# Decoder trunk on one core: means of squares as two products of a rounded part and the rest

## The chip, the cores and the metric

The kernel runs on one core of a Trainium2 chip. The metric is the device time of one execution in microseconds (us); lower is better. The names of the engines are those of the profile: PE (TensorE products), PEld (its weight loads), DVE (VectorE), ACT (ScalarE), POOL (GpSimd) and SP (the queue that issues most transfers).

## What is computed

One inference step of a one-layer decoder trunk, for a prompt of 256 tokens and eight samples of eight tokens each (320 columns in all). Everything is single precision at its borders:

```
h = RMSNorm(x); u = h @ w_in
y = x + (sigmoid(m_A) * (GDN(u) @ w_branch_a) + sigmoid(m_B) * (NSA(u) @ w_branch_b)) @ w_out
```

Mixer A (GDN) is a gated delta rule with 32 value heads. Mixer B (NSA) is sparse attention with 16 query heads and 4 key heads of 128: compressed blocks of keys, 16 selected blocks, and a window of 512. Two norms of mixer B matter here:

```
q  = rmsnorm(q_raw, q_norm_g)                               # 16 heads
kc = rmsnorm(compress(kc_full, pe_k, w_k, proj_k), k_gain)  # compressed keys
rmsnorm(x, g) = x * rsqrt(mean(x * x) + 1e-6) * g
```

## The kernel before

The 128 features of a head lie in the partitions, so a mean over features is a product with a 128x128 matrix of 1/128 on PE. A product can take plain single precision (F32) operands or F32R ones, rounded by ACT as they are written. The large projections take three F32R products a tile: weights rounded (`whi`) by the input rounded (`hhi`), `whi` by the input's rest (`hlo`), and the weights' rest (`wlo`) by `hhi`. They write `acc`. There are 11952 of them, and they are called the **fillers** below, since the order puts them wherever PE would wait.

The work comes in stages: (1) the norm of x and tables; (2) `prepare` (queries and keys of prompt and samples), `compressed` (the compressed keys of the eight samples, one after the other), `prompt` and `window`; (3) the selected blocks of the samples, in two streams (`sample`, called here the sample stage), which reads 256 pages of 256 KB as `spg`; (4) the delta rule, begun by `g_init`, which loads `c_gdn`, `c_gini` and others; (5) the last projections. The streams are generators. `Run` picks at each step the stream that a clock of estimated costs (`Clock`, `Timed`) lets start first, and so fixes, while the program is built, one order of instructions for each engine. The engines then run their own lists in that order, held by semaphores.

Projections wait in a list `Q`. `p_load` brings weights (`wraw`, three buffers) by SP, `p_hi` rounds them on ACT (`whi`), `p_lo` takes the rest on DVE (`wlo`), and `p_mm` makes the products. Until stage 3 is over, `Q` holds 99 column tiles of 48 products, 4752 fillers. The projections of the delta rule are put on the list only when the last sample is done, and after them, in the program's order, `g_init` starts.

`rstd` is the generator that both norms call. With `exact` set (16 query heads of 320 columns in `prepare`; eight samples of 512 columns in `compressed`) it multiplies the F32 `mean` by the F32 squares, in one product, and puts one Newton step behind. Without it (eight heads of other keys, one product of the prompt's compressed keys) it rounds the squares on ACT (`sqh`), takes the rest on DVE (`sql`), and makes two F32R products with `meanr`.

Of the kernel before, what the change touches and what calls it, by code (L numbers as in the profile page):

```python
# [10 lines left out]
F32 = mybir.dt.float32  # L11
F32R = mybir.dt.float32r
I32 = mybir.dt.int32
AF = mybir.ActivationFunctionType
OP = mybir.AluOpType
# [6 lines left out]
P = 128  # L22
# [424 lines left out]
def step(ctx: ExitStack, tc: tile.TileContext, I, O):  # L447
# [3 lines left out]
    V, S, G_, T, SY = (Timed(e, n, clock) for e, n in ((nc.vector, "dve"), (nc.scalar, "act"), (nc.gpsimd, "pool"), (nc.tensor, "pe"), (nc.sync, "sp")))  # L451
# [4 lines left out]
    def pool(cx, name, bufs=1, space=None, **kw):  # L456
        if space is not None:
            kw["space"] = space
        return Pool(cx.enter_context(tc.tile_pool(name=name, bufs=bufs, **kw)), name, bufs, clock, space is PSUM)
# [162 lines left out]
    for ti, (t0, n) in enumerate(TT):  # L622
# [3 lines left out]
        if ti == 0:  # L626
            K = load_pack(const, "const")
            ident, mean, one = K["ident"], K["mean"], K["one"]
    meanr = const.tile([P, P], F32R, name="meanr")
# [235 lines left out]
    for nm in ("k_win", "v_win"):  # L865
        G_.dma_start(O["p_" + nm][0, :256].rearrange("(a t) g d -> t a (g d)", a=2), zero)

    def rstd(pl, pp, tag, src, n, exact, tags=("sq", "rs", "nt")):

        sq = pl.tile([P, n], F32, tag=tags[0], name="sq", bufs=1)  # L870
        yield ("act", src)
        S.activation(sq, src, AF.Square)
        if exact:
            yield "pe"
            ms = pp.tile([P, 512], F32, tag=tag, name="ms")
            T.matmul(ms[:, :n], mean, sq, start=True, stop=True)
        else:
            hi, lo = (pl.tile([P, n], F32R, tag=t, name=t, bufs=1) for t in ("sqh", "sql"))
            yield "act"
            S.activation(hi, sq, AF.Copy)  # L880
            yield "dve"
            V.tensor_tensor(lo, sq, hi.bitcast(F32), op=OP.subtract)
            yield ("pe", lo, Next(pp, tag))
            ms = pp.tile([P, 512], F32, tag=tag, name="ms")
            T.matmul(ms[:, :n], meanr, hi, start=True, stop=False)
            T.matmul(ms[:, :n], meanr, lo, start=False, stop=True)
        yield "act"
        r = pl.tile([P, n], F32, tag=tags[1], name="rs", bufs=1)
        S.activation(r, ms[:, :n], AF.Ln, bias=eps)
        yield "act"  # L890
        S.activation(r, r, AF.Exp, scale=-0.5)
        yield "dve"
        if exact:
            a, b = exact
            t = pl.tile([P, b - a], F32, tag=tags[2], name="nt", bufs=1)
            V.tensor_tensor(t, r[:, a:b], r[:, a:b], op=OP.mult)
            V.scalar_tensor_tensor(t, ms[:, a:b], EPS, t, op0=OP.add, op1=OP.mult)
            yield "dve"
            V.tensor_scalar(t, t, -0.5, 1.5, op0=OP.mult, op1=OP.add)
            V.tensor_tensor(r[:, a:b], r[:, a:b], t, op=OP.mult)  # L900
            yield "dve"
        return r
# [219 lines left out]
    cp = pool(c_ctx, "cp", side="right")  # L1122
    cps = pool(c_ctx, "cps", 2, PSUM, side="right")
# [62 lines left out]
    def qT(b, g):  # L1186
        return qs[:, b, 4 * g:4 * g + 4, :].rearrange("p h t -> p (h t)")

    def pooled(b, kv):
        pp = cps.tile([P, 512], F32, tag="a", name="pp")  # L1190
        for i in range(0, 4, 2):
            pg = []
            for _ in range(8):
                pg.append((yield from cfeed.get()))
            yield ("tiles", *pg)
            for k in range(8):
                j = k % 4
                T.matmul(pp[32 * j:32 * j + 32], Pk[:, kv, i + k // 4], pg[k], start=i + k // 4 == 0, stop=i + k // 4 == 3)
            if i == 0:
                for j in range(3):  # L1200
                    T.matmul(pp[32 * j:32 * j + 32], Pk[:, kv, 4], pg[j + 1], start=False, stop=False)
            cfeed.release(8)
        yield "dve"
        pl = cp.tile([P, 512], F32, tag="c0", name="pl", bufs=1)
        V.tensor_tensor(pl.rearrange("p (g d) -> p g d", g=4), pp.rearrange("p (g d) -> p g d", g=4),
                        bc(cb[:, kv], [[0, 4], [1, P]]), op=OP.add)
        yield ("pe", clock.last, Next(cps, "a"))
        tp = cps.tile([P, 512], F32, tag="a", name="tp")
        for g in range(4):
            T.transpose(tp[:, g * P:g * P + P], pl[:, g * P:g * P + P], ident)  # L1210
        yield "act"
        pt = cp.tile([P, 512], F32, tag="c1", name="pt", bufs=1)
        S.activation(pt, tp, AF.Copy)
        yield "pe"
        return pt

    def compressed():
        for b in range(B):
            pt = yield from pooled(b, 0)
            yield lambda: done["q"] == 16  # L1220
            yield ("pe", clock.last, Next(cps, "a"))
            kp = cps.tile([P, 512], F32, tag="a", name="kp")
            T.matmul(kp, proj[:, 0], pt, start=True, stop=True)
            rs = yield from rstd(cp, cps, "a", kp, 512, (0, 512), ("c0", "c2", "c3"))
            kc = cp.tile([P, 512], F32, tag="c0", name="kc", bufs=1)
            V.scalar_tensor_tensor(kc, kp, gains[:, 1:2], rs, op0=OP.mult, op1=OP.mult)
            yield ("tiles", clock.last, Next(cps, "a"))
            sc = cps.tile([P, 512], F32, tag="a", name="sc")
            for g in range(4):
                T.matmul(sc[32 * g:32 * g + 32, :127], qT(b, g), kc[:, g * P:g * P + 127], start=True, stop=True)  # L1230
            yield "dve"
            s1 = cp.tile([P, 127], F32, tag="s1", name="s1")
            V.scalar_tensor_tensor(s1, sc[:, :127], SCALE, cmpB[:, :127], op0=OP.mult, op1=OP.add)
            mx = cp.tile([P, 3], F32, tag="mxc", name="mxc")
            V.tensor_reduce(mx[:, 0:1], s1, axis=AX.X, op=OP.max)
            V.tensor_scalar(mx[:, 0:1], mx[:, 0:1], -1.0, None, op0=OP.mult)
            yield "act"
            S.activation(s1, s1, AF.Exp, bias=mx[:, 0:1], accum_out=mx[:, 1:2])
            yield "dve"
            V.reciprocal(mx[:, 2:3], mx[:, 1:2])  # L1240
            V.tensor_scalar(s1, s1, mx[:, 2:3], None, op0=OP.mult)
            yield ("pe", clock.last, Next(cps, "a"))
            ip = cps.tile([P, 512], F32, tag="a", name="ip")
            q = 32 * (b % 4)
            T.matmul(ip[q:q + 32, :127], N["G"], s1, start=True, stop=True)
            T.transpose(ip[:127, P:2 * P], s1, ident)
            yield "dve"
            V.tensor_copy(imp[q:q + 32, b // 4, :127], ip[q:q + 32, :127])
            sT = cp.tile([P, P], F32, tag="sT", name="sT")
            V.tensor_copy(sT[:127], ip[:127, P:2 * P])  # L1250
            if b % 4 == 3:
                yield from select(b // 4)
                done["sel"] = b // 4 + 1
            pt = yield from pooled(b, 1)
            vp = cps.tile([P, 512], F32, tag="a", name="vp")
            for g in range(4):
                T.matmul(vp[:, g * P:g * P + P], pt[:, g * P:g * P + P], proj[:, 1], start=True, stop=True)
            yield "dve"
            vc = cp.tile([P, 512], F32, tag="c0", name="vc", bufs=1)
            V.tensor_copy(vc, vp)  # L1260
            yield ("tiles", clock.last, Next(cps, "a"))
            oc = cps.tile([P, 512], F32, tag="a", name="oc")
            for g in range(4):
                T.matmul(oc[32 * g:32 * g + 32, :P], sT[:127, 32 * g:32 * g + 32], vc[:127, g * P:g * P + P], start=True, stop=True)
            yield "dve"
            add_o(oc, gS[:, 0, b:b + 1], b)
            done["cmp"] = b + 1
# [152 lines left out]
    def add_o(x, g, b):  # L1420

        if b in seen:
            V.scalar_tensor_tensor(osum[:, b], x[:, :P], g, osum[:, b], op0=OP.mult, op1=OP.add)
        else:
            V.tensor_scalar(osum[:, b], x[:, :P], g, None, op0=OP.mult)
        seen.add(b)

    run.add(prompt())
    run.add(compressed(), CR)
    run.go(lambda: done["names"])  # L1430
    p_ctx.close()
# [948 lines left out]
```

## Time and profile before

| | us |
|---|---|
| median of 3 runs | 2538.18 |
| lowest, highest | 2533.05, 2538.55 |
| profiled execution: its time | 2536.51 |
| profiled execution: its span, first to last instruction | 2534.7 |
| busy in that span: PE / PEld / DVE / ACT / POOL | 2504.5 / 2337.8 / 1636.3 / 1398.0 / 414.1 |

The profile gives the busy time of each engine. The start of one product is also the moment at which PE took it up, so what a product costs PE is read from start to start; its own duration overlaps with the next. Time that PE stands idle is 30.2 us of the span.

### The profile page before, as it was taken

How to read it: one execution, taken by the hardware profiler on the slowest of the kernel's cores; microseconds unless marked ns; L12 is line 12 of the kernel's file. 1: busy time of each engine (PE TensorE's matmuls, PEld its weight loads, DVE VectorE, ACT ScalarE, POOL GpSimd, SP SyncE). 2: the span in 40 equal slices, each digit the busy share in tenths (PEclk: the TensorE clock that was granted, in tenths of full speed). 3: DMA queues.
4: the chain of work that ended last, by engine and by line, in shares of the span. 5: the costliest groups of instructions: out<-in, count | busy, mean ns of one | idle time of the engine just before them, and what ended most of it. 6: DMA issues, size and time to landing. Idle time of an engine off the chain costs nothing.

```text
span 2534.7 us, 59791 instructions
## 1 busy us (share of the span) xinstructions
PE 2504.5 (99%) x22405; PEld 2337.8 (92%) x22405; DVE 1636.3 (65%) x4075; ACT 1398.0 (55%) x3268; POOL 414.1 (16%) x992
## 2 busy tenths in 40 slices
PE   9999999999999999999999998999999999999999
PEld 8898789888888999999999998999999989999999
DVE  5554446655665555545888878889787876555543
ACT  4553444443444444435778776877877765544443
POOL 2000001000000000001223233433323432000000
PEclk9999999999999999999999999999999999999999
DMA  7657776888886999967455554554665556666564
GB/s 217 236 160 247 243 253 218 291 304 287 308 267 221 328 316 324 314 213 227 140 166 176 184 172 133 181 181 155 185 185 165 168 187 220 217 182 188 182 197 128
DMA packets 553827, 549.15 MB, mean 217 GB/s; under 512 B 33009, under 2 KB 457138, under 8 KB 553154
## 3 DMA queue, kind: packets, MB, share of 16 engines
q1 hardware_dynamic: 538690, 496.30, 61.4%
q0 software_dynamic: 14848, 49.04, 5.4%
q8 instruction: 177, 2.90, 0.5%
q14 instruction: 112, 0.92, 0.1%
HBM read 472.93 MB, written 72.29 MB: 215 GB/s over the span
## 4 chain that ended last, share of the span: by engine, by line
PE 89%; DVE 4%; issue 3%; DMA 2%; ACT 1%; POOL 1%; SPq 0%; DVEq 0%; ACTq 0%; POOLq 0%
PE acc L331 64%; PE ps L331 6%; PE nt L331 4%; PE op L331 3%; PE pp L331 3%; PE ns L331 2%; PE tp L331 2%; PE sp L331 1%; PE bank L331 1%; PE p L331 1%; PE pu L331 1%; PE ms L331 1%; POOL vx L331 1%; DVE wlo L331 1%; PE nought L331 0%
## 5 line engine op out<-in xcount | busy, mean ns | idle before, releaser
L331 PE MATMUL acc<-hhi,whi 128*128 128x320 f32 (+1 forms) x3472 | 1141.3, 329 | 0.6 <-ACT hhi L331 0.6
L331 PE MATMUL acc<-hlo,whi 128*128 128x320 f32 (+1 forms) x3472 | 1073.0, 309 | 1.2 <-DVE hlo L331 1.0
L331 PE MATMUL acc<-hhi,wlo 128*128 128x320 f32 (+1 forms) x3472 | 1073.8, 309 | 0.1
L331 ACT ACTIVATE whi<-wraw 128x512 fp32r<-128x512 f32 (+1 forms) x996 | 625.6, 629 | 812.7 <-PE acc L331 760.1
L331 DVE TENSOR_TENSOR wlo<-wraw,whi 128x512 fp32r<-128x512 f32 x992 | 682.1, 691 | 515.1 <-ACT whi L331 494.6
L331 PEld LDWEIGHTS acc<-hhi,whi 128*128 128x128 f32 (+1 forms) x3472 | 654.4, 188 | 25.1 <-issue 17.0
L331 PEld LDWEIGHTS acc<-hlo,whi 128*128 128x128 f32 (+1 forms) x3472 | 654.7, 189 | 8.7 <-issue 2.4
L331 PEld LDWEIGHTS acc<-hhi,wlo 128*128 128x128 f32 (+1 forms) x3472 | 652.2, 188 | 0.0
L331 PE MATMUL acc<-oah,whi 128*128 128x320 f32 x512 | 158.2, 309 | 0.0
L331 PE MATMUL acc<-oal,whi 128*128 128x320 f32 x512 | 158.2, 309 | 0.0
L331 PE MATMUL acc<-oah,wlo 128*128 128x320 f32 x512 | 158.2, 309 | 0.0
L331 POOL CAST vx<-v 32x128 fp32r<-32x128 f32 x256 | 94.9, 371 | 125.7 <-DVE v L331 88.5
L331 DVE SCALAR_TENSOR_TENSOR cv<-xp,cw,cv 128x344 f32<-128x344 f32 x192 | 110.0, 574 | 8.2 <-ACT cv L331 5.9
L299 POOL DMA_DIRECT2D d_mz<-raw x48 | 26.4, 550 | 493.7 <-ACT raw L331 411.6
L331 PEld LDWEIGHTS acc<-oah,whi 128*128 128x128 f32 x512 | 96.1, 188 | 0.0
L331 PEld LDWEIGHTS acc<-oal,whi 128*128 128x128 f32 x512 | 96.1, 188 | 0.0
L331 PEld LDWEIGHTS acc<-oah,wlo 128*128 128x128 f32 x512 | 96.1, 188 | 0.0
L331 ACT ACTIVATE kT<-nt 128x512 f32<-128x512 f32 x80 | 46.8, 594 | 82.1 <-PE nt L331 81.6
L331 DVE SCALAR_TENSOR_TENSOR sS<-sS,ends,pu 128x128 f32<-128x128 f32 x256 | 84.2, 338 | 11.3 <-PE pu L331 10.4
L331 DVE COPY kT<-nt 128x512 f32<-128x512 f32 x80 | 54.4, 689 | 51.1 <-PE nt L331 50.1
L331 PE MATMUL pp<-cpg,Pk 128*32 128x512 f32 x608 | 76.6, 597 | 0.0
L331 PE MATMUL nt<-pk_const,spg 128*128 128x128 f32 x512 | 73.3, 275 | 2.7 <-DMA spg<-cache_k_sel 2.7
(428 smaller groups left out, 3428.4 us busy)
## 6 DMA issues: line engine op xcount, KB each, us to landing
wraw<-w_in SPq DMA_DIRECT2D x120, 1024.0 KB
wraw<-w_in SPq DMA_DIRECT2D x129, 512.0 KB
cpg<-cache_k_cmp SPq DMA_DIRECT2D x128, 256.0 KB
cpg<-cache_v_cmp SPq DMA_DIRECT2D x128, 256.0 KB
spg<-cache_k_sel SPq DMA_DIRECT2D x128, 256.0 KB
spg<-cache_v_sel SPq DMA_DIRECT2D x128, 256.0 KB
wraw<-w_branch_a SPq DMA_DIRECT2D x32, 1024.0 KB
sS<-state_gdn SPq DMA_DIRECT2D x32, 512.0 KB
```

The lines of the kernel that those rows point to most:

```text
L299: return f(*a, **k)
L331: return f(*a, **k)
```

## The change

`rstd` always takes the way with two F32R products; `exact` now only says which columns get the Newton step. The compressed keys hand in names of buffers that are already there (`c2`, `c3`) for the rounded squares and the rest.

```diff
-    def rstd(pl, pp, tag, src, n, exact, tags=("sq", "rs", "nt")):
+    def rstd(pl, pp, tag, src, n, exact, tags=("sq", "rs", "nt", "sqh", "sql")):
...
-        if exact:
-            yield "pe"
-            ms = pp.tile([P, 512], F32, tag=tag, name="ms")
-            T.matmul(ms[:, :n], mean, sq, start=True, stop=True)
-        else:
-            hi, lo = (pl.tile([P, n], F32R, tag=t, name=t, bufs=1) for t in ("sqh", "sql"))
...
+        hi, lo = (pl.tile([P, n], F32R, tag=t, name=t, bufs=1) for t in tags[3:])
+        yield "act"
+        S.activation(hi, sq, AF.Copy)
+        yield "dve"
+        V.tensor_tensor(lo, sq, hi.bitcast(F32), op=OP.subtract)
+        yield ("pe", lo, Next(pp, tag))
+        ms = pp.tile([P, 512], F32, tag=tag, name="ms")
+        T.matmul(ms[:, :n], meanr, hi, start=True, stop=False)
+        T.matmul(ms[:, :n], meanr, lo, start=False, stop=True)
...
-            rs = yield from rstd(cp, cps, "a", kp, 512, (0, 512), ("c0", "c2", "c3"))
+            rs = yield from rstd(cp, cps, "a", kp, 512, (0, 512), ("c0", "c2", "c3", "c2", "c3"))
```

Since the order follows from estimated costs, the change moves instructions on every engine up to the start of the delta rule; from the product with `gg` on (the second that reads the table `pk_gini`) the order on PE is the same in both. Counted in the two orders, the fillers that stand ahead of four places on PE are:

| place on PE | fillers ahead, before | fillers ahead, now |
|---|---|---|
| first `mp` (start of the sample stage) | 3516 | 3744 |
| last `tp` of `o` (end of the sample stage) | 4659 | 4752 |
| `bank` of `bag` (first use of `pk_gini`) | 4782 | 4788 |
| `bank` of `gg` | 4818 | 4818 |

PE at the end of the sample stage, before. `ns` are scores, `nt` transposes of the softmax `xs`, `op` products with pages `spg`, `tp` the last transpose, `c4` a constant of the delta rule.

```order
L331 MATMUL op_15794<-spg_15944,pT_15994 32x128 x4
L331 MATMUL op_15794<-spg_15946,pT_15994 32x128 x4
L331 MATMUL acc_15851<-hhi_84,whi_15852 128x320
...
L331 MATMUL acc_16017<-hhi_84,wlo_15914 128x320
L331 MATMUL tp_16023<-pk_const_108,o_16012 128x128
L331 MATMUL acc_16017<-hhi_84,whi_15906 128x320
...
L331 MATMUL acc_16233<-hhi_84,wlo_16186 128x320
L331 MATMUL bank_16076<-pk_const_108,c4_16197 128x64 x4
```

The same place now:

```order
L331 MATMUL nt_16413<-pk_const_108,xs_15855 64x128
L331 MATMUL nt_16418<-pk_const_108,xs_15855 128x128 x4
...
L331 MATMUL op_16412<-vsS_135,pTn_16415 32x128 x4
L331 MATMUL op_16412<-spg_16028,pT_16423 32x128 x4
...
L331 MATMUL nt_16487<-pk_const_108,xs_15855 128x128 x4
...
L331 MATMUL op_16412<-spg_16485,pT_16508 32x128 x4
L331 MATMUL tp_16528<-pk_const_108,o_16526 128x128
L331 MATMUL acc_16577<-hhi_84,whi_16586 128x320
L331 MATMUL acc_16577<-hlo_85,whi_16586 128x320
...
L331 MATMUL bank_16565<-pk_const_108,c4_16606 128x64 x4
```

Before, fillers stand between the last scores of the last sample and its last transpose in seven places (48, 6, 3, 21, 18, 21 and 6 of them), and 111 between that transpose and `c4`. Now 27 stand behind the last scores, none from the first `nt` of `xs` to the last transpose, and 24 between that and `c4`; the first of these 24 is made of `whi_16586`, which ACT rounds from `wraw_16578`.

SP at the same place, before:

```order
L299 DMA wraw_15689<-w_in 128x8x128 x2
L299 DMA wraw_15823<-w_in 128x8x128 x2
L299 ISA
L299 DMA spg_15887<-cache_v_sel 128x512
...
L299 DMA spg_15946<-cache_v_sel 128x512
L299 DMA d_ob_73<-obS_9849 128x16x64
L299 DMA wraw_16088<-w_in 128x8x128 x2
L299 DMA wraw_16123<-w_in 128x8x128 x2
...
L299 DMA pk_gini_16205<-c_gini 128x640
```

and now:

```order
L299 DMA wraw_15734<-w_in 128x8x128 x2
...
L299 DMA spg_16483<-cache_v_sel 128x512
...
L299 DMA spg_16485<-cache_v_sel 128x512
L299 DMA d_ob_73<-obS_10301 128x16x64
L299 DMA wraw_16578<-w_in 128x8x128 x2
L299 DMA wraw_16581<-w_in 128x8x128 x2
...
L299 DMA pk_gini_16614<-c_gini 128x640
```

Six page loads stand between the last weights of the old list and `d_ob` before, 37 now. `wraw_16578`, which the first filler behind the last transpose needs, stands behind `d_ob` of `obS`, the result of that transpose.

## Rows read from the trace of the kernel before

**Rows 1.** The page, busy time, share of the span and instructions of each engine.

```profile
PE 2504.5 (99%) x22405; PEld 2337.8 (92%) x22405; DVE 1636.3 (65%) x4075; ACT 1398.0 (55%) x3268; POOL 414.1 (16%) x992
```

**Rows 2.** Windows: stretch, length, busy us by engine (instructions), TensorE's granted clock, DMA share, GB/s.

```profile
0.00:818.00 818.00, 812.45 (x6300) 712.07 (x6300) 463.33 (x1137) 363.82 (x779) 63.03 (x105) 1.00 0.75 250
818.00:1134.00 316.00, 313.29 (x3929) 293.99 (x3929) 169.49 (x278) 129.00 (x224) 14.62 (x31) 1.00 0.90 302
1134.00:1154.40 20.40, 18.82 (x130) 18.26 (x128) 11.06 (x23) 7.38 (x14) 1.77 (x5) 1.00 0.89 274
```

**Rows 3.** Timeline of PE, a query head's product: start us, us, operation.

```profile
83.43 0.70 PE L331 MATMUL ms<-sq,pk_const 128*128 128x320 f32 x2
83.72 0.55 PE L331 MATMUL acc<-hhi,whi 128*128 128x320 f32 x1
84.11 0.31 PE L331 MATMUL acc<-hlo,whi 128*128 128x320 f32 x1
```

**Rows 4.** Timeline of PE, the product of a sample's compressed keys.

```profile
183.11 1.02 PE L331 MATMUL ms<-sq,pk_const 128*128 128x512 f32 x2
...
184.11 0.31 PE L331 MATMUL acc<-hlo,whi 128*128 128x320 f32 x1
```

**Rows 5.** Timeline of PE, two F32R products of another key head.

```profile
276.11 0.31 PE L331 MATMUL ms<-sqh,meanr 128*128 128x320 f32 x1
276.26 0.31 PE L331 MATMUL ms<-sql,meanr 128*128 128x320 f32 x1
276.41 0.31 PE L331 MATMUL acc<-hhi,whi 128*128 128x320 f32 x1
276.55 0.31 PE L331 MATMUL acc<-hlo,whi 128*128 128x320 f32 x1
```

**Rows 6.** Timeline of PE, an F32R product of 512 columns in the delta rule.

```profile
1352.73 0.39 PE L331 MATMUL pu<-vx,k 128*128 128x512 f32 x1
1352.97 0.30 PE L331 MATMUL acc<-hhi,whi 128*128 128x320 f32 x1
```

**Rows 7.** The page, groups: rounding on ACT, rest on DVE, 512 columns; busy, mean ns.

```profile
L331 ACT ACTIVATE whi<-wraw 128x512 fp32r<-128x512 f32 (+1 forms) x996 | 625.6, 629 | 812.7 <-PE acc L331 760.1
L331 DVE TENSOR_TENSOR wlo<-wraw,whi 128x512 fp32r<-128x512 f32 x992 | 682.1, 691 | 515.1 <-ACT whi L331 494.6
```

**Rows 8.** Timeline of all engines, the softmax of the last sample.

```profile
1108.07 1.08 PE L331 MATMUL ns<-kT,qs 128*32 128x128 f32 x32
...
1110.41 2.35 DVE L331 TENSOR_REDUCE mx<-xs 128x1 f32<-128x2112 f32 x1
...
1113.61 2.05 ACT L331 ACTIVATE xs<-xs,mx 128x2112 f32<-128x2112 f32 x1
...
1116.22 0.27 PE L331 MATMUL nt<-pk_const,xs 128*64 128x128 f32 x1
```

**Rows 9.** The chain of waits from 1100 to 1165 us: start us, us, what.

```profile
1131.05 1.88 PE op L331 x64
...
1134.01 0.11 PE tp L331
...
1141.28 0.70 DVE wlo L331
...
1147.30 7.02 DMA pk_gini<-c_gini
...
1154.36 0.43 PE bank L331 x2
```

**Rows 10.** Timeline of the SP queue, end of the sample stage: start us, us, transfers issued.

```profile
1101.06 1.02 SPq L299 DMA_DIRECT2D wraw<-w_in  x2
...
1122.54 5.14 SPq L299 DMA_DIRECT2D spg<-cache_v_sel  x6
1135.04 0.38 SPq L299 DMA_DIRECT2D d_ob<-obS  x1
1135.53 7.25 SPq L299 DMA_DIRECT2D wraw<-w_in  x5
1143.01 2.11 SPq L299 DMA_DIRECT2D c<-gdn_conv_w  x1
```

**Rows 11.** Windows, columns as in rows 2, around a stall in the delta rule.

```profile
2048.00:2052.00 4.00, 1.73 (x22) 0.91 (x21) 3.10 (x13) 2.14 (x8) 1.46 (x3) 0.87 0.62 179
2052.00:2056.00 4.00, 3.54 (x27) 3.19 (x28) 2.35 (x7) 2.92 (x8) 0.00 (x0) 0.50 1.03 356
2056.00:2060.00 4.00, 3.98 (x26) 3.79 (x25) 2.66 (x10) 1.15 (x5) 0.00 (x0) 0.78 0.11 38
```

More of the change, by code (lines that the diff above doesn't have):

```diff
@@ L872, in rstd @@
         S.activation(sq, src, AF.Square)
-        if exact:
-            yield "pe"
-            ms = pp.tile([P, 512], F32, tag=tag, name="ms")
-            T.matmul(ms[:, :n], mean, sq, start=True, stop=True)
-        else:
-            hi, lo = (pl.tile([P, n], F32R, tag=t, name=t, bufs=1) for t in ("sqh", "sql"))
[L879 to L886, printed above, removed]
+        hi, lo = (pl.tile([P, n], F32R, tag=t, name=t, bufs=1) for t in tags[3:])
[7 more added lines that the diff above has]
+        T.matmul(ms[:, :n], meanr, lo, start=False, stop=True)
         yield "act"
```

## The prediction

> **What bounds the kernel now.** I read the page's busy times first: PE is busy 2504.5 of 2534.7 us, DVE 65% and ACT 55% of the span [rows 1]. That alone says only that PE is the first suspect, so the windows come next: PE works 812.5 of the first 818 us, 313.3 of the 316 us of the sample stage, and 18.8 of the 20.4 us between that stage and the first use of `pk_gini` [rows 2]. PE is the bound in every stage, because fillers stand in its list wherever something else is late. So two things can move the time: what PE has to do, and where it finds no filler. The diff tells only of the first, the order tells of the second.
>
> **What the products save.** A filler's pace is 276.55 less 276.41, about 0.147 us [rows 5]. A plain product of 320 columns, with the filler behind it, takes from 83.43 to 84.11 us, 0.68 us, so it alone costs 0.53 [rows 3]. Two F32R products of the same size take from 276.11 to 276.41, 0.30 us [rows 5]. Sixteen heads save 16 x 0.23 = 3.7 us. The plain product of 512 columns costs 184.11 less 183.11 less 0.147 = 0.85 us [rows 4]; an F32R product of 512 columns takes 0.24 us [rows 6], two of them 0.48, and eight samples save 8 x 0.37 = 3.0 us. Together **6.7 us** of PE, 0.26% of the span. Both terms could be off by a tenth: the trace rounds to 0.01 us.
>
> **What is added elsewhere.** 24 roundings on ACT and 24 subtractions on DVE, at most 0.63 and 0.69 us each [rows 7], so at most 15.1 and 16.6 us spread over some 700 us, in which ACT is busy 364 and DVE 463 of 818 us [rows 2]. I cost them at nothing: the fillers cover them, as they cover the same two steps of the eight other key heads. If that cover were gone, each head would cost its 1.3 us. What they do change is the order. Each sample's compressed keys now take two more steps, and the list comes out with 228 more fillers ahead of the sample stage (3744 for 3516) and 93 more ahead of its end (4752 for 4659).
>
> **What that does to the end of the sample stage.** 4752 is the whole list: when the last sample's softmax comes, no filler is left, where before 123 stood between its scores and its last transpose and 111 behind it. Five terms follow.
>
> 1. *More fillers ahead of the last transpose:* 93 x 0.147 = **+13.7 us**, and with the 6.7 us saved, +7.0. PE was never without work here [rows 2], so this is real time.
> 2. *The last softmax in the open.* Before, the scores end at 1109.15, the maximum takes 2.35 us on DVE, the exponential 2.05 on ACT, and the transposes start at 1116.22 [rows 8]: 7.1 us, filled with 48 fillers. Now 27 stand there, 4.0 us, so about 3 us are bare. After that PE alternates between transposes and products with pages. The last six pages are asked for only as earlier ones are released, over 5.14 us from 1122.54 [rows 10], and their products ran at 1131.05 [rows 9], with 18 and 21 fillers between. Without these 39 (5.7 us) I take another 4 us of waiting. Together **+7 us**. The bounds are 3 us, the softmax alone, and 14 us: all 96 fillers that are gone from between scores and transpose.
> 3. *From the last transpose to the first use of `pk_gini`.* This was a chain of transfers already, and PE waited at its end: transpose at 1134.01, `d_ob` issued at 1135.04, weights until the table is issued at 1147.30, and 7.02 us to its landing, product at 1154.36 [rows 9, 10], 20.3 us in all. The order on SP is the same, so PE gets there no earlier, though it now has only 36 fillers (5.3 us) in place of 123 (18.0 us). The stretch stays, its cover goes: PE idles some 12 to 14 us in place of about 1.6 [rows 2]. The chain itself can get a little shorter: SP held back weights until `wlo` had freed a buffer at about 1142 [rows 9], and now all three buffers are free. Without waits five issues take 2.6 us, an estimate from 1.02 us for the two halves of an earlier load, against 7.25 [rows 10]; some of these 4.6 us is the queue's own backlog. I take **-3 us**, with bounds of 0 and -4.6.
> 4. *Fewer fillers behind:* 36 before and 30 now between the products with `bag` and `gg`, 6 x 0.147 = **-0.9 us**.
> 5. From `gg` on the order is the same to the last row, so the delay is handed on whole: **0**.
>
> The sum: -6.7 + 13.7 + 7 - 3 - 0.9 = **+10.1 us**. On the profiled execution, whose time is 2536.5 us, that gives 2546.6. That execution lies 1.7 us below the median of the runs, 2538.2, on which I set the forecast: **2548 us**. The bounds of terms 2 and 3 alone give +4.5 to +20.1 us, 2543 to 2558.
>
> **The clock.** While PE idles, its clock can fall. The trace shows it: in a stretch of 4 us in which PE was busy for 1.73 us the granted clock began to fall from 1.00 (its mean was 0.87), in the next it was 0.50, the level of 1.2 GHz, and in the one after that 0.78 on its way back [rows 11]. In term 3 the 36 fillers can start some 10.8 us after the transpose, an estimate from rows: 1.0 to `d_ob`, 1.5 for the issues, 7.0 for the landing as with `pk_gini`, 1.3 for rounding and rest [rows 7, 9, 10]. At full pace they end at 16.1 us, inside the 17.3 that the chain takes; all of them at half pace end at 21.4. I take 0 us, since a fall lasted shorter than that, with +4 us as the other bound. The Trainium skill, TensorE: Matmul & The Clock Gate, section "Why this matters for your kernels", says to leave no idle gaps between bursts of products, or the clock goes back to half. By that rule, with which the rows agree, the fillers behind the gap would start at half pace, and the sum would be up to 4 us larger.
>
> **The rivals.**
>
> *The saving alone, and the time falls by 6.7 us, to 2531.5.* The mechanism: the 93 fillers and the bare tail cost nothing, because the sample stage is paced by its pages and not by PE. For it: the transfers are busy 0.90 of the stage at 302 GB/s [rows 2], the highest share of the three stretches. Then fewer fillers inside the stage (1008 for 1143) don't shorten it, PE had waits that the fillers only filled, and its end would come as early as the pages allow. Against it: PE idles 2.7 of 316 us in that stage [rows 2], and the fillers moved ahead of it are 33 us of work that has to be done first. It decides if terms 1 and 2 together come to less than about 5 us in place of 20.7.
>
> *The pages hold PE up, and the time rises by some 20 us, to 2558.* The stage keeps its 256 pages but has 135 fewer fillers, 19.8 us less of work on PE, and 45 fewer pieces of weights of 64 KB, 2.9 MB. At 302 GB/s [rows 2] the 95.4 MB of before less 2.9 take 306 us; PE would be through in 296. If that rate is the ceiling, PE waits 10 us more for pages. For it: the share of 0.90, and 37 page loads in a row on SP behind the last weights. Against it: a share below 1.
>
> *Nothing to be measured.* Terms 2 and 3 at their low ends and a little more off term 2 leave less than 5 us. There is no mechanism of its own for it; it is the low end of the forecast.
>
> **How the numbers follow.** A measurement of this kernel can tell 0.2%, about 5 us, from no change. The forecast has 0.65; some 0.14 of that falls under +5 us, by the low bounds of terms 2 and 3. The pages as the bound have 0.20, all slower. The saving alone has 0.15; 0.12 of it is faster by over 0.2%, the rest is not, should a part of the tail show. Together faster 0.12, same 0.17, slower 0.71. The range runs from 2533, which leaves out most of the saving alone, to 2562, the pages as the bound with the clock on top. The forecast's own range is 2543 to 2558.
>
> **What would show it right or wrong.** In the profile of the changed kernel: two products `ms` with `meanr` 0.30 us from filler to filler for a head, and about 0.48 for a sample. PE idle between the last scores of the last sample and its last `tp`, some 7 us in one or two waits, on ACT `xs` or DVE and on `spg`. Then the largest idle stretch of PE ahead of the end, 7 us or more, between that `tp` and the next filler, ended by `whi` or `wlo` behind a load of `wraw`, and a second wait that `pk_gini` ends. The transpose some 14 us later than at 1134.01, the product with `bag` some 11 us later than at 1154.36, and from there on nothing but this shift. I am wrong if the transpose comes at the old time or before; if the idle stretch behind it is short, because weights were there; if PE waits many times for `spg` inside the sample stage (then the pages were the bound); or if the stretch from `gg` to the end takes less time than before and gives the shift back.

## The result, and the profile after

The changed kernel takes **2549.05 us** (median of 6 runs, 2546.33 to 2552.24), the kernel before in the same comparison 2537.26 (6 runs, 2533.05 to 2539.55). The ratio is **1.0051**, with a 95% interval of 1.0042 to 1.0061: slower by some 12 us. The profiled execution of the changed kernel took 2547.34 us, with a span of 2545.5; the forecast was 2548 and, for that execution, 2546.6.

The page first, busy time, share of the span and instructions of each engine, beside [rows 1]:

```profile
PE 2502.0 (98%) x22405; PEld 2337.0 (92%) x22405; DVE 1647.7 (65%) x4099; ACT 1408.5 (55%) x3292; POOL 413.6 (16%) x992
```

PE is busy 2.5 us less than before, in a span that is 10.8 us longer. It stands idle for 43.5 us, before for 30.2. ACT and DVE have 24 instructions more each, and 10.5 and 11.4 us more work.

The products themselves, in the timeline of PE (start us, us, operation): those of a query head, and those of a sample, where `c` is the buffers `c2` and `c3`. They answer to [rows 3 to 5].

```profile
84.12 0.31 PE L331 MATMUL ms<-sqh,meanr 128*128 128x320 f32 x1
84.27 0.31 PE L331 MATMUL ms<-sql,meanr 128*128 128x320 f32 x1
84.42 0.31 PE L331 MATMUL acc<-hhi,whi 128*128 128x320 f32 x1
...
181.81 0.62 PE L331 MATMUL ms<-c,meanr 128*128 128x512 f32 x2
182.27 0.30 PE L331 MATMUL acc<-hhi,whi 128*128 128x320 f32 x1
```

Two products take 84.42 less 84.12, 0.30 us, for a head, and 0.46 for a sample, as foretold (0.30 and 0.48).

Now the windows, cut at the same places of the program in both kernels: first `mp`, end of the last scores, last `tp`, first product with `pk_gini`, end. Columns as in [rows 2], with `PEclk`, DMA share and GB/s last. The first two lines are of the kernel before, which [rows 2] show as one stretch; the others are of the changed kernel.

```profile
818.00:1109.15 291.15, 288.44 (x3652) 270.57 (x3651) 157.89 (x260) 118.95 (x206) 13.53 (x29) 1.00 0.94 315
1109.15:1134.00 24.85, 24.85 (x278) 23.42 (x279) 11.60 (x19) 10.05 (x18) 1.08 (x2) 1.00 0.50 149
```

```profile
0.00:841.80 841.80, 837.77 (x6530) 742.17 (x6530) 487.21 (x1180) 388.68 (x826) 66.03 (x110) 1.00 0.74 248
841.80:1131.10 289.30, 283.56 (x3613) 264.84 (x3612) 154.75 (x255) 115.88 (x201) 12.81 (x27) 1.00 0.93 309
1131.10:1147.60 16.50, 11.95 (x181) 8.84 (x181) 5.65 (x10) 3.94 (x6) 0.54 (x1) 0.99 0.34 107
1147.60:1165.60 18.00, 9.52 (x41) 8.44 (x41) 7.60 (x18) 4.30 (x8) 0.14 (x2) 0.63 0.89 271
1165.60:2545.50 1379.90, 1359.16 (x12045) 1312.67 (x12045) 992.50 (x2637) 895.73 (x2252) 334.04 (x852) 1.00 0.57 177
```

Each stretch against before, in us. What the fillers make of it is their number times 0.147, and the products stand at the 6.7 us that were foretold; the rest is what is left of the change of its length:

| stretch | before | after | change | fillers, change | their time | products | rest |
|---|---|---|---|---|---|---|---|
| start to first `mp` | 818.0 | 841.8 | +23.8 | +228 | +33.5 | -6.7 | -3.0 |
| to the end of the last scores | 291.2 | 289.3 | -1.9 | -39 | -5.7 | | +3.8 |
| to the last `tp` | 24.9 | 16.5 | -8.3 | -96 | -14.1 | | +5.8 |
| to `bank` of `bag` | 20.4 | 18.0 | -2.4 | -87 | -12.8 | | +10.4 |
| to `bank` of `gg` | 5.8 | 4.9 | -0.9 | -6 | -0.9 | | 0 |
| to the end | 1374.6 | 1375.0 | +0.4 | 0 | 0 | | +0.4 |

The columns of fillers and products sum to -6.7 us, the saving alone; the rest sums to +17.4; together that is 10.7 us, the 10.8 of the span with rounding. So the fillers that went ahead of the sample stage were not given back behind it. The waits of PE say who was late (what waits, for what: us in total, times, longest):

```profile
PE acc L331 <- ACT whi L331: 6.8, 1, 6.8
PE nt L331 <- DMA spg<-cache_k_sel: 5.7, 7, 1.7
...
PE op L331 <- DMA spg<-cache_v_sel: 2.2, 5, 1.4
...
PE nt L331 <- ACT xs L331: 1.9, 1, 1.9
```

The first is the largest wait of the whole run; it stands behind the last transpose. For `spg` PE waited 2.7 us before, in two waits, and now 7.9 in twelve. The chain of waits shows the place (start us, us, what), as [rows 8, 9] did:

```profile
1132.30 2.37 DVE mx L331
...
1142.05 4.64 DMA spg<-cache_v_sel
...
1146.73 0.47 PE op L331 x8
...
1147.63 0.49 PE tp L331
...
1148.96 5.23 DMA wraw<-w_in
1154.21 1.16 ACT whi L331 x2
1155.37 0.24 SPq L299
...
1159.46 6.12 DMA pk_gini<-c_gini
...
1165.62 0.43 PE bank L331 x2
```

Maximum (`mx`) and exponential of the last softmax, then the last pages, then the first weights behind the last transpose, then the table: each link was in the program before, with fillers beside it. The SP queue in the same place, beside [rows 10]:

```profile
1148.47 0.38 SPq L299 DMA_DIRECT2D d_ob<-obS  x1
1148.96 6.65 SPq L299 DMA_DIRECT2D wraw<-w_in  x5
1155.83 1.51 SPq L299 DMA_DIRECT2D c<-gdn_conv_w  x1
...
1159.46 0.43 SPq L299 DMA_DIRECT2D pk_gini<-c_gini  x1
```

### The profile page after: what moved, and what is told of

Same layout as the page of the kernel before. It is cut to its first block, busy times and chain, and to the rows that moved or that the text cites. A ratio compares the mean times of both kernels' runs of the same rounds, so it can differ in the third digit from the quotient of the medians.

```text
span 2545.5 us, 59837 instructions
## 1 busy us (share of the span) xinstructions
PE 2502.0 (98%) x22405; PEld 2337.0 (92%) x22405; DVE 1647.7 (65%) x4099; ACT 1408.5 (55%) x3292; POOL 413.6 (16%) x992
## 4 chain that ended last, share of the span: by engine, by line
PE 90%; DVE 4%; DMA 3%; ACT 1%; issue 1%; POOL 1%; SPq 1%; DVEq 0%; ACTq 0%; POOLq 0%
PE acc L331 65%; PE ps L331 6%; PE nt L331 3%; PE pp L331 3%; PE op L331 3%; PE tp L331 2%; PE ns L331 2%; PE sp L331 1%; DMA spg<-cache_k_sel 1%; PE bank L331 1%; PE p L331 1%; DVE wlo L331 1%; PE pu L331 1%; POOL vx L331 1%; PE ms L331 0%
## 5 line engine op out<-in xcount | busy, mean ns | idle before, releaser
L331 DVE SCALAR_TENSOR_TENSOR sS<-sS,ends,pu 128x128 f32<-128x128 f32 x256 | 84.5, 340 | 10.8 <-PE pu L331 10.0
```

The lines of the kernel that those rows point to most:

```text
L331: return f(*a, **k)
```

## The experiments

**The theory**: the 24 means are cheaper on PE and their new steps are covered, but the cover comes out of a list that then runs out at the end of the sample stage; the order carries the loss. **The rivals**: the saving doesn't reach the end of the program at all; the work added on ACT and DVE is the loss; the pages of the sample stage are. Each comparison has its own runs of the kernel before (medians 2535.5 to 2536.4), so ratios are compared across them, and 0.001 is 2.5 us.

### Runs 1 and 2: products and order apart

`ghost` charges the planner's clock and issues nothing, `T.eng` issues and charges nothing. So the order on every engine stays that of the kernel from which the run starts. Run 1 is made of the kernel before, run 2 of the changed one.

```diff
-        sq = pl.tile([P, n], F32, ...)
+        sq = pl.tile([P, n], F32R if exact else F32, ...)
...
-            T.matmul(ms[:, :n], mean, sq, start=True, stop=True)
+            ghost.matmul(ms[:, :n], mean, sq.bitcast(F32), start=True, stop=True)
+            for _ in range(2):
+                T.eng.matmul(ms[:, :n], meanr, sq, start=True, stop=True)
```

```diff
+        if exact:
+            ghost.matmul(ms[:, :n], meanr, hi, start=True, stop=False)
+            ghost.matmul(ms[:, :n], meanr, lo, start=False, stop=True)
+            T.eng.matmul(ms[:, :n], mean, sq, start=True, stop=True)
```

> The kernel before with its own order of instructions to the last row, in which the 24 plain products are replaced: ACT writes the squares rounded, and two F32R products with meanr read them, the second in place of the first. The rest of the squares is left out, so no rounding and no subtraction is added, and the means are those of rounded squares. My theory (the products save 6.7 us, the order loses more): 2537.3 - 6.7 = 2530.5, from 2529 to 2533. If the saving is hidden, because transfers and not PE pace these stages, or because two F32R products cost what a plain one does: 2537, as before.

> The changed kernel with its own order of instructions to the last row, in which the 24 means are one plain product of the unrounded squares again; rounding and rest are computed and not used. My theory: the order alone carries the loss, so the saving is missing on top of it: 2549.05 + 6.7 = 2556, from 2554 to 2558. If the products save nothing that reaches the end: 2549. If the added roundings and subtractions on ACT and DVE hold the products up, this kernel, whose products don't wait for them, is faster than the changed one: under 2547.

Run 1: 2527.09 us, ratio 0.9968 (0.9956 to 0.9979), 8 us faster than before. Run 2: 2554.49 us, ratio 1.0071 (1.0057 to 1.0084), 5 us over the changed kernel's 1.0051 (1 to 9, by the two intervals). Where the products stand, the traces say it more sharply: up to the first `mp` run 1 is 8.6 us ahead of the kernel before (809.4 for 818.0 us), and run 2 8.0 behind the changed kernel (849.8 for 841.8), each pair with the same order. So the products save what was foretold or a little more, in either order, and it reaches the end: that rival falls. The new order with the old products is 18 us slower than the old order with them. That figure is not the order alone, since run 2 also makes the 24 roundings and rests; run 6 asks for their price. Run 2's largest waits of PE are those of the changed kernel, the one behind the last transpose among them:

```profile
PE nt L337 <- DMA spg<-cache_k_sel: 6.8, 6, 2.4
PE acc L337 <- ACT whi L337: 6.7, 1, 6.7
```

### Runs 5 and 6: what rounding and rest cost without cover

Both keep the order of before. Run 5 puts the whole change where the plain product stood; run 6 adds the two steps to run 1, and no product waits for them. The diff is run 5's.

```diff
+            hi, lo = (pl.tile([P, n], F32R, tag=t, name=t, bufs=1) for t in tags[3:])
+            S.eng.activation(hi, sq, AF.Copy)
+            V.eng.tensor_tensor(lo, sq, hi.bitcast(F32), op=OP.subtract)
...
+            T.eng.matmul(ms[:, :n], meanr, hi, start=True, stop=False)
+            T.eng.matmul(ms[:, :n], meanr, lo, start=False, stop=True)
```

> The whole change (rounding, rest, two products that wait for the rest) in the order of the kernel before, to the last of its old rows: the three new steps stand where the plain product stood, with no filler put between them. The saving of 6.7 us against 2536 gives 2529.5; on top comes what the 24 waits for rounding and rest cost with no cover of their own, at most 24 x 1.3 = 31 us, so up to 2561. If it comes out over 2549, the new order's 228 fillers ahead of the sample stage (33 us of work) were well spent and the loss is the price of these waits. If it comes out under 2549, the new order spends more cover than the waits are long, and the loss is one of the planner's, not of the change itself: I expect this, at 2540, since the products wait behind fillers in a list in which PE is rarely early.

> The first run (two products of rounded squares in the order of before) with the 24 roundings and 24 subtractions put back on ACT and DVE at the same place, but with nothing that waits for them: the products read the rounded squares, the rest is left out of the means. My theory, in which ACT and DVE have room there and PE's cover hides them: as the first run, 0.9968 of before, within 2 us (2525 to 2530). If the added work on these two engines is what the changed kernel pays: up to 15 us more than the first run, 2540.

Run 5: 2564.21 us, ratio 1.0112 (1.0097 to 1.0128). Run 6: 2533.99 us, 0.9996 (0.9987 to 1.0005). I had expected about 2540 and 2527, and both miss, on the same side; run 6 lies in its second case, in which the added work is paid. Against run 1 the steps of run 5 and the waits for them cost 0.0144, 36.5 us, 1.5 us for each product; and steps that no product waits for cost 0.0028, 7 us (3 to 11), by themselves. Whether these 7 are a part of the 36.5 wasn't tried. The windows up to the first `mp`, of runs 1, 5 and 6 (columns as above), put nearly all of it there:

```profile
0.00:809.40 809.40, 804.16 (x6300) 710.16 (x6300) 463.27 (x1137) 362.15 (x779) 62.86 (x104) 1.00 0.75 253
```

```profile
0.00:844.00 844.00, 817.10 (x6302) 711.59 (x6302) 474.79 (x1161) 374.46 (x803) 62.92 (x105) 1.00 0.73 242
```

```profile
0.00:815.60 815.60, 805.71 (x6302) 709.51 (x6302) 475.12 (x1161) 373.12 (x803) 62.93 (x105) 1.00 0.75 251
```

844.0 less 809.4 is 34.6 us, 815.6 less 809.4 is 6.2. In run 6 PE idles 9.9 us there, in run 1 5.2; the new waits are short ones for other steps of the two engines, the longest of 1.4 us for `pc` of DVE. Nor is it true that nothing at all waits for the new steps: in two of the samples ACT's `rs` waits for the rest, 1.1 us together, since `rs` takes over the buffer that the rest still reads. One bare head in the timeline of run 5, of ACT, DVE and PE by their start, shows why (in brackets the idle time of the engine before it, and who ended it):

```profile
84.53 0.47 ACT L337 ACTIVATE sq<-raw 128x320 f32<-128x320 f32 x1
...
85.30 0.63 ACT L337 ACTIVATE whi<-wraw 128x512 fp32r<-128x512 f32 x1 [0.30 <-PE acc L337]
85.84 0.45 ACT L884 ACTIVATE sqh<-sq 128x320 fp32r<-128x320 f32 x1
86.32 0.49 DVE L885 TENSOR_TENSOR sql<-sq,sqh 128x320 fp32r<-128x320 f32 x1 [1.43 <-ACT sqh L884]
86.34 0.41 PE L888 MATMUL ms<-sqh,meanr 128*128 128x320 f32 x1 [0.93 <-ACT sqh L884]
86.87 0.41 PE L889 MATMUL ms<-sql,meanr 128*128 128x320 f32 x1
```

The square starts at 84.53 and ends at 85.00. The rounding starts at 85.84 only, since a `whi` stands ahead of it in ACT's list, itself held back 0.30 us by PE. PE idles 0.93 us for it, and the second product follows 0.53 us behind the first, where two of them take 0.15 each when nothing is late. The first `mp` of run 5 comes at 844.0 us, 2 us behind that of the changed kernel, which by then has done 228 fillers more, 33.5 us of work. So the fillers stand where PE would really have waited: I had expected a planner that spends more cover than the waits are long, and as a price of all 228 that is wrong. As a price of the last of them it is not: run 8 below has 108 fillers fewer ahead of the first `mp`, 15.9 us of work, and comes there 11.9 us earlier, so that these 108 saved only 4.0 us of waits. The new steps cost some 36 us of PE's time where the order gives them nothing; this order gives them 33.5 us of fillers, and that of run 8 17.6.

### Runs 3 and 4: more work on the list

```diff
-NM = 3
+NM = 1
```

> The changed kernel with two more slabs of weights (192 fillers) on the list ahead of the sample stage, in place of behind the projections of the delta rule: 4875 fillers now stand ahead of the last transpose and 114 between it and the product with bag (123 before, 36 in the changed kernel). My theory: the end of the sample stage is covered again, the saving of 6.7 us shows: 2531, from 2528 to 2535. If the added work on ACT and DVE is the loss: 2549. If the pages are the bound: it stays near 2549, or gets less by the few us that the stage's own fillers move.

> The control of the run before: the same two slabs moved to the list ahead of the sample stage in the kernel before. It had 123 fillers behind the last transpose and a covered tail, and the count of both hardly changes, so my theory expects no change: 2537, from 2534 to 2539. If moving these slabs is good in itself, whatever the products are, it falls as much as the run before does.

Run 3: 2547.12 us, 1.0037 (1.0024 to 1.0051). Run 4: 2543.84 us, 1.0031 (1.0020 to 1.0043). Both miss: 2531 and 2537 were expected. The last transpose did become covered, with no wait of PE for `xs` or for `whi` (3.6 us are left behind it, for a constant and for `wlo`), but the control shows what the two slabs are worth where they were taken from: it is 8 us slower than before. And against this control the change is worth nothing, 1.0037 for 1.0031, though the tail is covered in both. Run 3 reaches the first `mp` 24.3 us behind run 4 with 33.5 us of fillers more ahead of it, so up to there it is 9 us better; from there to `gg` it loses 11, with 7.3 us of waits for `spg`, where run 4 has 2.4. So a covered tail was not enough. The waits of PE between 1960 and 2160 us, in the last part of the delta rule, in run 3 and then in run 4; before, the wait for `hhi` in the same stretch came to 0.6 us:

```profile
PE acc L331 <- ACT hhi L331: 3.9, 3, 2.1
```

```profile
PE acc L331 <- ACT hhi L331: 4.5, 3, 2.3
```

Cover taken from the delta rule opens waits there: from 2000 to 2040 us PE has 141 fillers and works 39.5 of 40 us before, and 84 and 28.8 in run 4. Fillers are a fixed stock, and these two slabs were in use where they stood.

### Run 7: the next weights early

The projections of the delta rule are put on the list before the last samples are done; their products are held.

```diff
+    NG, NXP, pos = 16, 4, {"open": 0, "xp": 0, "xc": 0}
...
-        ok = lambda f: pos["xp"] - pos["xc"] < NXP
+        ok = lambda f: pos["open"] and pos["xp"] - pos["xc"] < NXP
...
     run.go(lambda: done["sample"] == 3)
     nsa_ctx.close()
...
+    pos["open"] = 1
```

> The changed kernel with the projections of the delta rule put on the list before the last samples are done, held at the product until the sample stage is over, so that their first weights are loaded and rounded during its tail. The list still ends at 4752 ahead of the last transpose, but 102 fillers stand ready between it and the product with c4 in place of 24. My theory: the wait of 6.8 us for rounded weights behind the last transpose goes, the tail ahead of it is bare by some 4 us more (no filler stands in it now, 27 before): 2546, from 2542 to 2549. If that wait only moves to the table, because the chain of transfers to pk_gini sets that stretch: 2549 to 2553.

2573.15 us, ratio 1.0143 (1.0129 to 1.0157), far worse than either theory said. The run can't be read as a whole, since the order of the delta rule changed with it and its waits on PE grew (those for `TTd` from 1.9 to 6.2 us): from `gg` to the end it takes 1389.3 us, 14 more than the changed kernel, with 81 fillers fewer. Its chain of waits at the place in question can be read:

```profile
1156.54 0.47 PE tp L331
1157.01 8.26 PE acc L331 x47
1165.29 0.64 ACT whi L331
...
1170.90 5.64 DMA pk_gini<-c_gini
...
1176.58 0.43 PE bank L331 x2
```

The wait of 6.8 us for rounded weights is gone, and the product with `bag` comes 20.0 us behind the transpose (18.0 in the changed kernel). PE is busy for 18.7 of them, with 111 fillers in place of 36, and waits 1.4 us for the table, so this stretch does get its cover. But the fillers now stand in the chain themselves: 47 of them run before ACT can round the next weights, then DVE takes the rest, and only then SP goes on (it waited 8.4 us for `wlo`); the table is issued 14.4 us behind the transpose, in the changed kernel 11.8. So the second theory, that the transfers set this stretch whatever PE does, isn't shown: here PE's own work held the transfers up.

### Runs 8 and 9: the end covered from within the stage

```diff
-HOLD, STICK = 3000, 400
+HOLD, STICK = 2000, 200
```

Run 8 makes this edit in the changed kernel, run 9 in the kernel before.

> The changed kernel with two constants of the planner changed (how long a stream waits to gather narrow products, 3000 to 2000 ns, and how much later a wide one must be, 400 to 200 ns), so that the planner spends less of the list early: 3636 fillers stand ahead of the sample stage (3744 in the changed kernel, 3516 before), 108 between last scores and last transpose (27, 123), 108 between that and the product with c4 (24, 111). My theory: with the end of the stage covered, the saving shows: 6.7 us under the control that follows, so 2530, from 2527 to 2536. If the waits for rounding and rest cost PE real time wherever the list stands: 2541 or more, 5 us or more over the control.

> The control: the same two constants in the kernel before. The counts of fillers at the five places come out the same as in the run before, 3636, 108 and 108 among them, so the two differ in the 24 means alone. My theory expects little change against before, since its tail was covered and is covered: 2536, from 2533 to 2542 (PE changes 38 times more often between fillers and other work). If these constants are good in themselves it falls by as much as the run before does.

Run 8: **2533.35 us**, ratio 0.9992 (0.9983 to 1.0001), some 15 us under the changed kernel and not to be told from before. Run 9: 2541.24 us, 1.0025 (1.0014 to 1.0036), 5 us over before. With the same counts of fillers at the five places, the change is worth 0.9992 against 1.0025: 8 us faster. The traces put it where the products are: the first `mp` comes at 829.9 us in run 8 and at 837.3 in run 9, 7.4 us apart, with 3636 fillers ahead in both. Against the kernel before, whose planner has the old constants, nothing is gained.

```profile
0.00:829.90 829.90, 826.11 (x6422) 727.05 (x6422) 480.89 (x1171) 381.81 (x815) 65.35 (x108) 1.00 0.75 249
```

```profile
0.00:837.30 837.30, 832.63 (x6420) 728.34 (x6420) 469.28 (x1147) 370.88 (x791) 64.01 (x108) 1.00 0.74 247
```

The windows of run 8 behind that, cut at the places of those of the changed kernel above (the second cut stands 0.5 us behind the end of the scores):

```profile
829.90:1112.80 282.90, 277.12 (x3562) 257.50 (x3562) 154.69 (x254) 114.05 (x197) 12.52 (x26) 1.00 0.95 319
1112.80:1134.80 22.00, 22.00 (x259) 20.35 (x258) 10.25 (x17) 9.14 (x16) 1.08 (x2) 1.00 0.47 143
1134.80:1153.50 18.70, 18.57 (x127) 18.04 (x126) 10.38 (x23) 7.33 (x13) 1.23 (x4) 1.00 0.86 266
```

PE idles 0 of 22.0 us from the last scores to the last transpose (4.6 of 16.5 in the changed kernel), and 0.1 of 18.7 from there to `bag` (8.5 of 18.0). The page waits inside the stage are left, 5.2 of the 5.8 us that PE idles there (4.6 in run 9). What the edit costs by itself, run 9 shows but doesn't explain; that PE changes more often between narrow and wide products is a guess.

### Runs 10 to 12: fewer fillers spent

Run 10 (changed kernel) and run 12 (kernel before) have `HOLD, STICK = 1000, 400`, run 11 (changed kernel) 2000, 400.

> The changed kernel with one constant changed (3000 to 1000 ns of gathering): 3576 fillers ahead of the sample stage, 108 between the last scores and the last transpose, 120 between that and the product with c4, and 17 switches between narrow and wide products fewer ahead of the delta rule than there were in e8 by my count of runs of such products (329 for 359; 311 in the kernel before, 321 in the changed one). My theory: the end is covered, the saving shows, and fewer switches cost less: 2531, from 2527 to 2536. If 57 more fillers left over at the end of the stage mean that PE waited earlier without them: 2536 to 2544.

> The changed kernel with 2000 ns of gathering and the old 400 ns: 3588 fillers ahead of the sample stage, 108 and 111 at its end, 353 switches. My theory: covered as in e8, so 2533, from 2529 to 2538. If fillers that are left over mean that PE waited earlier: 2537 to 2545.

> The control of e10: 1000 ns of gathering in the kernel before: 3522 fillers ahead of the sample stage, 108 and 108 at its end, 353 switches. Here the counts differ from those of e10 by 54 ahead of the stage, so that the pair is not as clean as e8 and e9. My theory: the control lies over e10 by the saving or a little less, at 2537, from 2534 to 2543. If the constant is good in itself, it falls under before by as much as e10 does.

(By the figures of the first text the switches are 359 less 329, 30 fewer.) Run 10: 2542.62 us, 1.0021 (1.0011 to 1.0031). Run 11: 2540.74, 1.0017 (1.0008 to 1.0026). Run 12: 2544.50, 1.0031 (1.0021 to 1.0041). Runs 10 and 11 are within the ranges of the second case and over those of my theory; run 12 is over the range of its theory by 1.5 us and doesn't fall, so both its cases miss. Run 10 lies 2.5 us under its control, which these runs can't tell from nothing. The first `mp` of run 10 comes 2 us earlier than in run 8, with 60 fillers, 8.8 us of work, fewer ahead of it: 7 us of the saving in cover came back as waits, such as the largest of run 10:

```profile
PE mp L331 <- DVE xn L331: 3.9, 1, 3.9
```

Right behind this wait the granted clock is 0.50 too, in the 4 us from 828 in which PE works without a break. The table puts the pairs side by side: what is left of the change against the kernel before in three stretches, in us, fillers taken off at 0.147. In the kernels with the change the first column holds the products' saving, some -7 to -8.

| run | fillers ahead of first `mp` | start to first `mp` | first `mp` to `gg` | `gg` to the end |
|---|---|---|---|---|
| changed kernel | 3744 | -9.7 | +20.2 | +0.4 |
| 3, with the change | 3744 | -9.5 | +11.2 | +9.0 |
| 4, its control | 3516 | -0.3 | -0.1 | +8.4 |
| 8, with the change | 3636 | -5.7 | +3.7 | +0.1 |
| 9, its control | 3636 | +1.7 | +2.7 | -1.6 |
| 10, with the change | 3576 | +1.0 | +7.1 | +1.2 |
| 12, its control | 3522 | +2.0 | +4.5 | +0.1 |

Where many fillers stand ahead of the first `mp`, the saving is whole there and is lost behind it; where few do, it is lost ahead of it. Of these pairs only 8 and 9 keep most of it. The rows are of one execution each; those of run 10 lie 13.5 us apart, and the profiled one 3 us over their median, so its row is rough.

No version here beats the kernel before beyond what these runs can tell, apart from run 1, which leaves the rest of the squares out.

## Why the prediction was right

The time was right to 1 us. The mechanism was right too: the fillers run out, and the end of the sample stage lies bare. That the sum came so near is in part luck, for two terms were not seen and cancel, several terms were off by about 1 us, and one reason was wrong.

- **The products save 6.7 us.** Right. By rows 16 x (0.53 - 0.30) + 8 x (0.85 - 0.46) = 6.8 us; run 1 measured 8 us (5 to 11), runs 8 and 9 some 8, run 2 some 5; the three pairs of traces give 8.6, 7.4 and 8.0 up to the first `mp`, so 6.7 is a little low.
- **"I cost them at nothing: the fillers cover them."** Right in the sum, since term 1 has the price, and not to be read as free: bare, each product's rounding and rest cost 1.5 us (1.3 foretold), and in the old order they cost 7 us over the 24 even where no product waits for them. In an order made for them these 7 us don't show: run 8 keeps 7.4 us against run 9 up to the first `mp`. The cover that they take is what the change costs.
- **Terms 1 and 2** put the last transpose 14.0 us later; it came 13.6 later. The tail in the open was taken at 7 us and measured 5.8, with the waits at the softmax (1.9 us) and at `spg` (2.2) that were named. The two unseen terms cancel: up to the first `mp` the time rose 3.0 us less than fillers and products make it, and in the sample stage 3.8 us more. Some 1 us of the first is the products, which save more than 6.7.
- **The pages hold PE up** had 0.20, at 20 us. It is true in part: PE waits for `spg` twelve times instead of two, 5.2 us more, of which 3 us fall ahead of the last scores. By the prediction's own sign, many waits for `spg` inside the stage, the pages would be the bound; seven waits are many, but they come to 5.7 of 289.3 us. Nor was 302 GB/s a ceiling: up to the last scores the transfers ran at 315 before and at 309 now, and [rows 11] show 356 in one stretch.
- **Term 3** was taken at -3 us and measured -2.4, but for another reason. The five issues of weights were to shrink from 7.25 to 2.6 us since all buffers are free; they took 6.65. The rounding on ACT at 1154.21 is followed by the next issue on SP at 1155.37, so SP still held a load back for a buffer. The gain is the sum of small ones: 0.6 us there, 0.9 in the landing of `pk_gini` (6.12 for 7.02), and the remainder on SP. The idle time of PE in this stretch was to be 12 to 14 us and is 8.5: the first filler came 7.3 us behind the transpose and not 10.8 (the load took 5.23 us, taken at 7.0), and 21 fillers ran at half pace.
- **Terms 4 and 5**: -0.9 as foretold, and 0.4 us in 1375 where 0 was said.
- **The clock** was taken at 0, with a bound of +4. It fell, and it cost nothing. Windows of the changed kernel, columns as above:

```profile
1148.00:1152.00 4.00, 0.11 (x1) 0.00 (x0) 0.29 (x1) 0.00 (x0) 0.00 (x0) 0.50 0.57 134
1152.00:1156.00 4.00, 1.11 (x3) 0.88 (x4) 1.13 (x2) 1.15 (x2) 0.14 (x2) 0.50 1.13 330
1156.00:1160.00 4.00, 4.00 (x16) 4.00 (x16) 3.76 (x13) 1.77 (x3) 0.00 (x0) 0.50 1.12 366
1160.00:1164.00 4.00, 3.01 (x18) 2.71 (x18) 2.42 (x4) 0.63 (x1) 0.00 (x0) 0.87 0.73 249
```

With PE idle the granted clock is 0.50, the level of 1.2 GHz, and it stays there while fillers run back to back from 1156, 0.267 us from start to start in place of 0.147. They still ended in time: in the timeline of PE it then waits again, 0.99 us for `c` and 0.70 for `pk_gini`. The Trainium skill, TensorE: Matmul & The Clock Gate, section "Why this matters for your kernels", says to leave no such gap between bursts of products. The rows agree on the clock; what it costs depends on whether the burst behind the gap is what the program waits for, and here it was not.

What stays open: why the two constants cost 5 us by themselves in run 9, why run 3 loses in the sample stage what run 8 keeps, and how much of the sample stage's 3.8 us is the order of the page loads and how much their bandwidth.

## What to carry to other kernels

Where one list of independent work fills every wait, a step that is "hidden" is paid from that list: count what the cover is, and look where the list now ends. A cheaper product that needs two more steps ahead of it saved 7 us on PE and took 33 us of cover, and lost until the list was spent differently within the same stage; even then it only drew level with the kernel before, and won 8 us against a control that had lost 5. Cover moved in from elsewhere opened the waits there. Compare the order of the two programs before judging an operation, and test the two apart: new operation in the old order, old operation in the new one.

## What was not expected of the hardware

Work that no product waits for was not free on engines that are half idle: 24 roundings on ACT and 24 subtractions on DVE, of 0.47 and 0.49 us for a head, made the time 7 us longer (runs 6 and 1), with DVE busy 65% and ACT 55% of the span of the kernel before. The engines of this program run their lists in order, so a step that is ready also waits for what stands ahead of it, as the rounding of run 5 did behind a `whi`: 1.31 us from the start of the square to the start of the rounding, though the square took 0.47. In run 6 PE idles 4.7 us more than in run 1 up to the first `mp`, in short waits for other steps of the two lists. That this is the whole of the 7 us was not tried.
